# Half-size products in the gated projections of a decoder layer

## Chip, cores and metric

The kernel runs on one core of one Trainium2 chip. The metric is the device time of one execution in microseconds (us). The engines of the core work side by side, each through its own queue in order: PE (TensorE, matrix products), PEld (PE's loading of the stationary operand), DVE (VectorE), ACT (ScalarE), POOL (GpSimd) and SP (SyncE, which issues the loads and stores here). Times of single instructions come from one execution that the hardware profiler recorded.

## What is computed

One layer of a decoder on 512 tokens of width 1024, in float32:

```python
h = x + 0.5 * swiglu(rmsnorm(x, ffn1_norm), ffn1_w_in, ffn1_w_out)
h = h + hybrid_mixer(rmsnorm(h, mix_norm), ...)
h = h + 0.5 * swiglu(rmsnorm(h, ffn2_norm), ffn2_w_in, ffn2_w_out)
y = rmsnorm(h, final_norm)

def swiglu(x, w_in, w_out):            # w_in: 1024 x 5632, w_out: 2816 x 1024
    a, b = jnp.split(x @ w_in, 2, axis=-1)
    return (jax.nn.silu(a) * b) @ w_out
```

The mixer (two gated recurrences between a wide input projection and output projections) lies between the two feed-forward parts and isn't touched but for one argument.

## The kernel before

Activations lie transposed: 128 channels on the partitions, 512 tokens along a row. `h` is the residual stream in 8 such tiles. Each float32 product is made of three passes in a reduced float32 type: an operand is split into `hi` (a cast on ACT) and `lo` (operand minus `hi`, on DVE), and `mm3` (L165 to L168) multiplies hi by hi, hi by lo and lo by hi into one PSUM bank. For weights `slab` (L154) does it: SP loads 128 x 512 numbers into `raw` (3 buffers), ACT casts to `whi` (L161), DVE subtracts into `wlo` (L162), 6 buffers each. `dense` (L170) makes one block of 128 output channels from as many slabs as its depth needs: 2 slabs for 1024 channels, 24 matmuls of 512 columns.

`ffn` (L227) is called for both feed-forward parts. For each j of 22 it makes two blocks, pa and pb (the gate and the value columns of the split above), and then, on the way out of PSUM, multiplies both by `rbc` (the reciprocal root mean square of each token, L250 and L253), takes Silu of the first on ACT, multiplies them on DVE (L255) and splits the result at once into `gh` and `gl` (L256, L257). So the input of these products, `uh` and `ul`, is `h` times the norm's gain, not yet divided by the root mean square, and the statistics of a token may come late: the blocks of the first `late` pairs are made before `rbc` exists. Then 8 blocks of output follow, each from 22 tiles of gh and gl (66 matmuls), added to `h`, and `after` prepares the next norm (squares into `acc` on POOL, `uh`/`ul` of the mixer).

`opening` (L279) starts the first part with an order written out by hand (`tc.manual_schedule`): the 4 blocks of the first two pairs share their loads. `stats` (L207) sums the squares over the channels on PE, `root` (L221) takes the power -0.5 on POOL, and four small matmuls spread the result into `rbc`. Outside `manual_schedule` the build tool's own planner orders each engine's queue; the mixer, too, is written out by hand. `last` (L347) makes the last output block of the second part in two halves of 256 tokens and the final norm.

Of the kernel before, what the change touches and what calls it, by code (L numbers as in the profile page):

```python
# [16 lines left out]
P = 128  # L17
# [22 lines left out]
LATE = 1  # L40
WB = 6
EXTRA = ((1, 3, 5, 7), (1, 3, 5, 7), (1, 3, 5, 7), (5, 7))
# [82 lines left out]
def body(tc, xT, cst, sqc, hmask, dta, w1o, w1a, w2a, wt, wn, wab, wbh, wbg, wo, w1b, w2b, yT, dbg=None):  # L125
# [70 lines left out]
    def sqacc(kt, pl, tag="sqt", bufs=2, add=pool):  # L196
# [5 lines left out]
        act.activation(s, h[:, kt], AF.Square)  # L202
        if kt < KD - 1:
            add.tensor_tensor(acc, acc, s, op=ALU.add)  # L204
        return s

    def stats(pl, last, between=lambda: None):  # L207
        pt = psc.tile([P, T], F32, tag="pd", name="pst")
        for i in range(NT):
            c = slice(i * P, (i + 1) * P)  # L210
            pe.matmul(pt[:, i:i + 1], acc[:, c], ones[:, :1], start=True, stop=False)
            pe.matmul(pt[:, i:i + 1], last[:, c], ones[:, :1], start=False, stop=True)
        root(pl, pt[:, :4], rcol)
        between()
        pb = psc.tile([P, T], F32, tag="pd", name="pbc")
        for i in range(NT):
            pe.matmul(pb[:, i * P:(i + 1) * P], rcol[:, i:i + 1].to_broadcast([P, P]), ident,
                      start=True, stop=True)
        act.copy(rbc, pb)
# [7 lines left out]
    def ffn(w1, w2, c0, after, late=0, lead=None, last=None):  # L227
        with tc.tile_pool(name="ff", bufs=1) as fp:
            gh = fp.tile([P, KF, T], F32R, name="gh")
            gl = fp.tile([P, KF, T], F32R, name="gl")  # L230
            early, ahead = [], []
            if lead is not None:
                early, ahead = opening(w1, fp)
            for j in range(len(early) // 2, late):
                for n in ("fa", "fb"):
                    early.append(fp.tile([P, T], F32, name=n, bufs=3))
                    act.copy(early[-1], dense(w1[j, len(early) % 2 ^ 1], KD, ux))
            if lead is not None:
                lead()
            for j in range(KF):  # L240
                if j < late:
                    pa, pb = a, b = early[2 * j:2 * j + 2]
                    if lead is not None and j:
                        a, b = (fp.tile([P, T], F32, name=n, bufs=3) for n in ("fa", "fb"))
                    dve.tensor_tensor(a, pa, rbc, op=ALU.mult)
                    dve.tensor_tensor(b, pb, rbc, op=ALU.mult)
                else:
                    pa = ahead.pop(0) if ahead else dense(w1[j, 0], KD, ux)
                    a = fp.tile([P, T], F32, name="fa", bufs=3)
                    dve.tensor_tensor(a, pa, rbc, op=ALU.mult)  # L250
                    pb = ahead.pop(0) if ahead else dense(w1[j, 1], KD, ux)
                    b = fp.tile([P, T], F32, name="fb", bufs=3)
                    dve.tensor_tensor(b, pb, rbc, op=ALU.mult)  # L253
                act.activation(a, a, AF.Silu)
                dve.tensor_tensor(a, a, b, op=ALU.mult)  # L255
                act.copy(gh[:, j], a)  # L256
                dve.tensor_tensor(gl[:, j], a, gh[:, j].bitcast(F32), op=ALU.subtract)  # L257
            for d in range(KD if last is None else KD - 1):
                pt = dense(w2[d], KF, lambda k: (gh[:, k], gl[:, k]))
                dve.scalar_tensor_tensor(h[:, d], pt, 0.5, h[:, d], op0=ALU.mult, op1=ALU.add)  # L260
                after(d, fp)
            if last is not None:
                last(gh, gl, fp)

    def nextnorm(c0, spill=None, defer=False, **sqt):
        def after(d, pl):
            if spill is not None:
                sp.dma_start(spill[d], h[:, d])
            if c0 is not None:
                prep(d, c0)  # L270
            if defer and d == KD - 1:
                act.activation(rbc, h[:, d], AF.Square)
                return
            s = sqacc(d, pl, **sqt)
            if d == KD - 1:
                stats(pl, s)
        return after

    def opening(w, pl):  # L279

        with tc.manual_schedule(engines={x.engine for x in (pe, act, dve, pool, sp)}):
            raws = {}

            def fetch(eng, kt, c=slice(0, 512)):
                if kt not in raws:
                    raws[kt] = wp.tile([P, 512], F32, tag="raw", name="raw", bufs=RB)
                eng.dma_start(raws[kt][:, c], w1o[kt, :, c])
            act.dma_start(cs[:, :C_N], cst)
            fetch(act, 0, slice(0, 256))
            act.activation(rbc[:, :1], ones[:, :1], AF.Silu)  # L290
            sp.dma_start(h[:, 0], xT[:, 0])
            fetch(sp, 0, slice(256, 512))
            for kt in range(1, KD):
                sp.dma_start(h[:, kt], xT[:, kt])
                fetch(sp, kt)
                if kt == 4:
                    sp.dma_start(sq, sqc)

            pw = psc.tile([P, T], F32, tag="pe", name="pwarm", bufs=LANES["e"])
            for i in range(11):  # L300
                pe.matmul(pw[:, :P], ones, ones, start=True, stop=True)
            pts = [psd.tile([P, T], F32, tag="mm", name="pmm") for _ in range(2)]
            pts += [psc.tile([P, T], F32, tag="pa", name="pmm", bufs=LANES["a"]) for _ in range(2)]
            for kt in range(KD):
                prep(kt, C_F1)
                lo = wp.tile([P, 512], F32R, tag="wlo", name="wlo", bufs=WB)
                hi = wp.tile([P, 512], F32R, tag="whi", name="whi", bufs=WB)
                for c in (slice(0, 256), slice(256, 512)) if kt == 0 else (slice(0, 512),):
                    act.copy(hi[:, c], raws[kt][:, c])
                    dve.tensor_tensor(lo[:, c], raws[kt][:, c], hi[:, c].bitcast(F32), op=ALU.subtract)  # L310
                for o, pt in enumerate(pts):
                    c = slice(o * P, (o + 1) * P)
                    mm3(pt, hi[:, c], lo[:, c], uh[:, kt], ul[:, kt], kt == 0, kt == KD - 1)
                if kt:
                    sqacc(kt - 1, pl, add=dve)
            s = sqacc(KD - 1, pl)
            slabs = [slab(w[2, 0][:, :512])]
            out = []
            for pt, n in zip(pts, ("fa", "fb")):
                out.append(pl.tile([P, T], F32, name=n, bufs=3))  # L320
                act.copy(out[-1], pt)
            slabs.append(slab(w[2, 0][:, 512:]))

            more = []

            def half(n):
                if n % 2 == 0:
                    more.append(psd.tile([P, T], F32, tag="mm", name="pmm"))
                for i in range(4):
                    k, c = n % 2 * 4 + i, slice(i * P, (i + 1) * P)  # L330
                    mm3(more[-1], *(x[:, c] for x in slabs[n]), *ux(k), k == 0, k == KD - 1)

            def between():
                half(0)
                slabs.append(slab(w[2, 1][:, :512]))
            stats(pl, s, between)
            half(1)
            slabs.append(slab(w[2, 1][:, 512:]))
            half(2)
            half(3)  # L340
        return out + pts[2:], more
# [5 lines left out]
    def last(gh, gl, pl):  # L347

        scaled = (1, 3, 5)
        with tc.tile_pool(name="fo", bufs=1) as fo:  # L350
            for kt in scaled:
                act.activation(h[:, kt], h[:, kt], AF.Copy, scale=cs[:, C_FN + kt:C_FN + kt + 1])
            for q in range(2):
                c = slice(q * 256, q * 256 + 256)
                pt = dense(w2b[KD - 1], KF, lambda k: (gh[:, k, c], gl[:, k, c]), n=256)
                dve.scalar_tensor_tensor(h[:, KD - 1, c], pt[:, :256], 0.5, h[:, KD - 1, c], op0=ALU.mult, op1=ALU.add)
                s = fo.tile([P, 256], F32, name="s7", bufs=2)
                act.activation(s, h[:, KD - 1, c], AF.Square)
                ps_ = psc.tile([P, T], F32, tag="pd", name="pst")
# [4 lines left out]
                r = fo.tile([P, 2], F32, name="rl", bufs=2)  # L364
                root(fo, ps_[:, :2], r)
                pb = psc.tile([P, T], F32, tag="pe", name="pbc")
# [1321 lines left out]
```

## Time and profile before

| what | us |
|---|---|
| median of 3 runs | 1637.57 |
| lowest and highest | 1637.13, 1640.69 |
| the profiled execution | 1637.01 |
| its span, first to last instruction | 1635.2 |
| PE busy in the span | 1622.3 |
| DVE, ACT, POOL busy | 973.1, 702.1, 313.5 |
| granted TensorE clock, mean | 0.997 |

The span is what the profile's rows divide up; the execution's own time is 1.8 us longer. A row of the timeline is start, duration (us), engine, line of the kernel, operation, output<-inputs, shapes, count, and in brackets the idle time before it with what ended that. A row of a group is line, engine, operation, tiles and shapes with the count, then the busy time of the group in us and the mean of one in ns, then the idle time before them. Where a line is asked for by itself, its row gives the least, median and greatest duration in ns. A matmul's duration is longer than the distance to the next, since they overlap; the distance is its price. The first feed-forward part runs to about 370 us of the span, the mixer to about 1260, the second part from there to the end.

### The profile page before, as it was taken

The numbers are of one execution on the slowest core, as the hardware profiler recorded it, in microseconds if no ns is written. First come the engines' busy times: TensorE is split into PE (matmuls) and PEld (weight loads), VectorE is DVE, ScalarE is ACT, GpSimd is POOL, SyncE is SP. The second block draws the span as 40 slices with busy tenths as digits, with TensorE's granted clock in tenths as the row PEclk, the third lists the DMA queues.
The fourth block names the chain that finished last, engine by engine and source line by source line (L and its number), as shares of the span: only waits on it lengthen the run. The fifth ranks groups of instructions, "written<-read, shape, count | busy, mean of one in ns | idle before, by whom it ended". The sixth has DMA issues, their size and how long they took to land. (4 is left out here: it accounts for less than half of the span.)

```text
span 1635.2 us, 25919 instructions
## 1 busy us (share of the span) xinstructions
PE 1622.3 (99%) x9376; PEld 1346.7 (82%) x9376; DVE 973.1 (60%) x1961; ACT 702.1 (43%) x1582; POOL 313.5 (19%) x615
## 2 busy tenths in 40 slices
PE   9999999999999999999999999999999999999997
PEld 8888888888888888878888888888888888888886
DVE  5544443336787779758888887755544444444333
ACT  5333333323434345446666565554234433333232
POOL 0000000001221222256526656600002000000001
PEclk9999999999999999999999999999999999999998
DMA  5333333433312222443333234445634333333333
GB/s 171 111 97 97 97 94 110 118 110 97 92 53 72 85 85 91 125 146 97 97 104 123 85 110 127 138 145 181 187 107 136 95 98 97 98 97 91 97 100 103
DMA packets 107408, 178.48 MB, mean 109 GB/s; under 512 B 19584, under 2 KB 25472, under 8 KB 107280
## 3 DMA queue, kind: packets, MB, share of 16 engines
q1 hardware_dynamic: 106992, 176.60, 35.3%
q8 instruction: 74, 1.21, 0.3%
q14 instruction: 54, 0.44, 0.1%
q10 hardware_dynamic: 288, 0.22, 0.0%
HBM read 161.80 MB, written 14.97 MB: 108 GB/s over the span
## 5 line engine op out<-in xcount | busy, mean ns | idle before, releaser
L166 PE MATMUL pmm<-uh,whi 128*128 128x512 f32 x1400 | 567.6, 406 | 0.0
L168 PE MATMUL pmm<-uh,wlo 128*128 128x512 f32 x1400 | 547.0, 391 | 0.0
L167 PE MATMUL pmm<-ul,whi 128*128 128x512 f32 x1400 | 545.8, 390 | 0.0
L161 ACT CAST whi<-raw 128x512 fp32r<-128x512 f32 (+1 forms) x286 | 174.1, 610 | 392.7 <-PE pmm L167 373.8
L162 DVE TENSOR_TENSOR wlo<-raw,whi 128x512 fp32r<-128x512 f32 (+1 forms) x286 | 193.7, 678 | 239.9 <-ACT whi L161 239.6
L168 PEld LDWEIGHTS pmm<-uh,wlo 128*128 128x128 f32 x1400 | 262.8, 188 | 56.9
L166 PEld LDWEIGHTS pmm<-uh,whi 128*128 128x128 f32 x1400 | 263.2, 188 | 50.9
L167 PEld LDWEIGHTS pmm<-ul,whi 128*128 128x128 f32 x1400 | 263.5, 188 | 49.5 <-DVE ul L193 0.3
L1463 ACT CAST whi<-raw 128x512 fp32r<-128x512 f32 x226 | 140.5, 621 | 224.3 <-PE pmm L167 180.7
L1465 DVE TENSOR_TENSOR wlo<-raw,whi 128x512 fp32r<-128x512 f32 x226 | 158.6, 702 | 120.9 <-ACT whi L1463 119.3
L204 POOL TENSOR_TENSOR acc<-acc,sqt 128x512 f32<-128x512 f32 x18 | 23.3, 1297 | 774.0 <-ACT sqt L202 774.0
L166 PE MATMUL pmm<-gh,whi 128*128 128x512 f32 (+1 forms) x374 | 141.0, 377 | 0.0
L168 PE MATMUL pmm<-gh,wlo 128*128 128x512 f32 (+1 forms) x374 | 140.9, 377 | 0.0
L167 PE MATMUL pmm<-gl,whi 128*128 128x512 f32 (+1 forms) x374 | 140.8, 377 | 0.0
L168 PEld LDWEIGHTS pmm<-gh,wlo 128*128 128x128 f32 x374 | 70.4, 188 | 13.0
L166 PEld LDWEIGHTS pmm<-gh,whi 128*128 128x128 f32 x374 | 70.4, 188 | 12.9
L167 PEld LDWEIGHTS pmm<-gl,whi 128*128 128x128 f32 x374 | 70.4, 188 | 12.8
L813 DVE SCALAR_TENSOR_TENSOR cy<-ci,cs,cy 128x512 f32<-128x512 f32 x96 | 72.7, 761 | 3.2 <-ACT cy L810 2.0
L948 POOL TENSOR_TENSOR fm<-gfs,gln 128x60 f32<-128x60 f32 (+24 forms) x155 | 63.7, 411 | 55.4 <-DMA gln<-hmask 43.9
L949 POOL TENSOR_TENSOR gln<-gln,fm 128x60 f32<-128x60 f32 (+24 forms) x155 | 64.3, 415 | 12.1
L253 DVE TENSOR_TENSOR fb<-pmm,rbc 128x512 f32<-128x512 f32 x41 | 28.4, 692 | 62.3 <-PE pmm L168 62.3
L250 DVE TENSOR_TENSOR fa<-pmm,rbc 128x512 f32<-128x512 f32 x41 | 28.3, 691 | 59.7 <-PE pmm L168 59.7
(420 smaller groups left out, 2191.4 us busy)
## 6 DMA issues: line engine op xcount, KB each, us to landing
raw<-wt SPq DMA_DIRECT2D x160, 256.0 KB
raw<-w1b SPq DMA_DIRECT2D x88, 256.0 KB
raw<-w1a SPq DMA_DIRECT2D x80, 256.0 KB
raw<-w2b SPq DMA_DIRECT2D x45, 256.0 KB
raw<-w2a SPq DMA_DIRECT2D x40, 256.0 KB
raw<-wn SPq DMA_DIRECT2D x32, 256.0 KB
raw<-wbg SPq DMA_DIRECT2D x32, 256.0 KB
gb<-gtd SPq DMA_DIRECT2D x16, 256.0 KB
```

What stands on the lines that cost most here:

```text
L161: act.copy(hi[:, :f], raw[:, :f])
L162: dve.tensor_tensor(lo[:, :f], raw[:, :f], hi[:, :f].bitcast(F32), op=ALU.subtract)
L166: pe.matmul(pt, ah, bh, start=first, stop=False)
L167: pe.matmul(pt, ah, bl, start=False, stop=False)
L168: pe.matmul(pt, al, bh, start=False, stop=last)
L250: dve.tensor_tensor(a, pa, rbc, op=ALU.mult)
L253: dve.tensor_tensor(b, pb, rbc, op=ALU.mult)
L813: dve.scalar_tensor_tensor(y, ci[:, j:j + T], wc[j], y, op0=ALU.mult, op1=ALU.add)
L948: pool.tensor_tensor(tv, bc(m[:, j + 1:, j], w), t[:, j:j + 1, :w].to_broadcast([P, n, w]), op=ALU.mult)
L949: pool.tensor_tensor(t[:, j + 1:, :w], t[:, j + 1:, :w], tv, op=ALU.add)
L1463: act.copy(hi, raw)
L1465: dve.tensor_tensor(lo, raw, hi.bitcast(F32), op=ALU.subtract)
```

## The change

In both feed-forward parts most pairs (all but 4 in the first part, all but 3 in the second) are made in another way. The 256 output channels of a pair (128 of gate, 128 of value), the 1024 input channels and the 512 tokens are each cut in two, and the product of the two 2 x 2 block matrices is made by seven products of half size for eight (Winograd's form of Strassen's scheme). Each such product is 4 x 3 matmuls of 256 columns. For that

- POOL makes four sums of weight blocks a pair (`s1` to `s4`), and each of the seven weight operands is cast on ACT and subtracted on DVE;
- the seven operands on the token side are made once for each part (`operands`): the normalised input `xn` (gain and `rbc` applied), sums of its quarters, and their hi and lo;
- the products are put together on the way out of PSUM (`f0` to `f8`).

The gate's result stays in one float32 tile until the stage ends; then 17 of the 22 are cast and subtracted (`part`), into the room of the token-side operands. The other 5 are split at once into parts of `uh` and `ul`; in the first part POOL copies them away again (`move`) before the mixer's input is written there. Everything in `ffn` is now inside `manual_schedule`: `stream` runs over units (a product, or four depth tiles of an ordinary block) and issues each engine's work so many units ahead. The order of the pairs is `ORDER`; `w1o` is rearranged on the host to match. `stats` is split into `sums` and `spread`, which the stream calls between units. In the second part the statistics are taken inside the stream (`defer=True` in the mixer's last call).

```diff
-LATE = 1
 WB = 6
+RW, SW = 6, 4
+ORDER = [*range(4, 15), *range(16, 22), 0, 1, 2, 3, 15]
...
+    def stream(units, fp, early, hooks, posts):
...
+        def loads():
+            while waiting:
+                r = waiting[0]
+                n = sent[r.fast]
+                m = RW if r.fast else RB
+                if len(n) >= m and n[-m].left:
+                    break
+                r.tile = fp.tile([P, T], F32, name="rw", bufs=RW) if r.fast else \
+                    wp.tile([P, T], F32, tag="raw", name="raw", bufs=RB)
+                sp.dma_start(r.tile[:, :r.src.shape[-1]], r.src)
+                n.append(waiting.pop(0))
+
+        def ahead(comb, cast, low):
+            while todo["low"] < min(low, len(units)):
+                i = todo["low"]
+                x, hi, lo = parts[i]
+                dve.tensor_tensor(lo, x, hi.bitcast(F32), op=ALU.subtract)
+                for r in units[i].drop:
+                    r.left -= 1
+                todo["low"] += 1
+            loads()
+            while todo["comb"] < min(comb, len(units)):
+                if units[todo["comb"]].comb:
+                    units[todo["comb"]].comb()
+                    loads()
+                todo["comb"] += 1
+            while todo["cast"] < min(cast, len(units)):
...
+                act.copy(hi, x)
...
+        for t, u in enumerate(units):
+            for f in hooks.get(t, ()):
+                f()
+            u.run(*parts[t][1:])
+            for f in posts.get(t, ()):
+                f()
+            ahead(min(t, todo["cast"]) + WB + 3, min(t + WB + 1, todo["cast"] + 2), min(t + WB, todo["cast"]))
...
+    def fast(w, p, xo, fp, at, posts, gate):
...
+        def comb(n, x, y, op):
+            def f():
+                a, b = (z.tile if isinstance(z, Raw) else v[z] for z in (x, y))
+                v[n] = fp.tile([P, T], F32, name="sw", bufs=SW)
+                pool.tensor_tensor(v[n], a, b, op=op)
...
+        def sums(n, add, twice=False):
+            t, pt = fp.tile([P, T], F32, name=n, bufs=2 if n == "fa" else 1), v["pt"]
+            t2, p2, add = (x.rearrange("p (a t) -> p a t", t=256) for x in (t, pt, add))
+            dve.tensor_tensor(t2, p2, add.to_broadcast([P, 2, 256]) if twice else add, op=ALU.add)
+            return t
+        def f0():
+            act.copy(v["p1"], v["pt"][:, one[0]])
+        def f2():
+            v["ua"] = sums("fa", v["p1"], True)
+        def f3():
+            act.activation(v["ua"][:, one[1]], v["ua"][:, one[1]], AF.Silu)
+        def f4():
+            v["uu"] = sums("uu", v["ua"][:, one[0]], True)
+            dve.tensor_tensor(v["vb"], v["pt"][:, one[1]], v["uu"][:, one[0]], op=ALU.add)
+        def f6():
+            v["uc"] = sums("uc", v["uu"])
+        def f7():
+            act.activation(v["uc"][:, one[1]], v["uc"][:, one[1]], AF.Silu)
+        def f8():
+            gate(p, (ua[:, one[1]], uc[:, one[1]]), (uc[:, one[0]], v["vb"]))
...
+        return [
+            Unit([a11, a21], raw(a11), prod(0, 0, "m"), drop=(a11,)),
+            Unit([a22, a12], of("s2"), prod(2, 0, "a"), lambda: (s1(), s2())),
+            Unit([], raw(a12), prod(3, 1), drop=(a12,)),
+            Unit([], of("s1"), prod(1, 1, "b")),
+            Unit([], of("s3"), prod(4, 0), comb("s3", a11, a21, ALU.subtract)),
+            Unit([], of("s4"), prod(5, 1, "m"), comb("s4", a12, "s2", ALU.subtract)),
+            Unit([], raw(a22), prod(6, 0), drop=(a22,))]
...
+    def operands(c0, xs, rooms, start, hooks):
...
+        scaled = lambda k: lambda: dve.scalar_tensor_tensor(xn[:, k], h[:, k], cs[:, c0 + k:c0 + k + 1], rbc,
+                                                            op0=ALU.mult, op1=ALU.mult)
+        work = ((scaled(0), scaled(1)), (scaled(2), scaled(3), less(pool, t1, b12, b11)),
+                (high(0), scaled(4), scaled(5)), (scaled(6), scaled(7), low(0)),
+                (less(pool, b12, b22, b12), less(dve, t2, b22, t1), high(3), high(2)), (low(2), low(3), high(1)),
+                (low(1), less(pool, t2, b21, t2), high(4)), (low(4), high(5)), (low(5), high(6)), (low(6),))
...
+            for p in range(17):
+                on(end - 6 + p if p < 6 else end + (p - 6) // 3, part(p))
...
-    ffn(w1a, w2a, C_F1, nextnorm(C_MX, hd, defer=True), late=2, lead=lead)
+    ffn(w1a, w2a, C_F1, nextnorm(C_MX, hd, defer=True), 4, lead=lead)
...
-    ffn(w1b, w2b, C_F2, nextnorm(None), late=LATE, last=last)
+    ffn(w1b, w2b, C_F2, nextnorm(None), 3, last=last)
...
-        e["nextnorm"](C_F2, tag="ta", bufs=TA)(d, mp)
+        e["nextnorm"](C_F2, defer=True, tag="ta", bufs=TA)(d, mp)
```

`hooks` are called before a unit's matmuls are issued, `posts` behind them. In `fast`, `at` is the pair's first unit, and `f0` to `f8` are posts of the units `at` to `at + 8`, so the last two fall into the next pair. `work` in `operands` is spread over ten units from unit 2 (first part) or 3 (second part) on.

More of the change, by code (lines that the diff above doesn't have):

```diff
@@ L205, in sqacc, with stats, sums, spread @@
         return s
[L207 to L219, printed above, removed]
+    def stats(pl, last):
+        def sums():
+            pt = psc.tile([P, T], F32, tag="pd", name="pst")
+            for i in range(NT):
+                c = slice(i * P, (i + 1) * P)
+                pe.matmul(pt[:, i:i + 1], acc[:, c], ones[:, :1], start=True, stop=False)
+                pe.matmul(pt[:, i:i + 1], last[:, c], ones[:, :1], start=False, stop=True)
+            root(pl, pt[:, :4], rcol)
+        def spread():
+            pb = psc.tile([P, T], F32, tag="pd", name="pbc")
+            for i in range(NT):
+                pe.matmul(pb[:, i * P:(i + 1) * P], rcol[:, i:i + 1].to_broadcast([P, P]), ident,
+                          start=True, stop=True)
+            act.copy(rbc, pb)
+        return sums, spread
     def root(pl, ss, out):
@@ L273, in after @@
                 return
-            s = sqacc(d, pl, **sqt)
-            if d == KD - 1:
-                stats(pl, s)
-        return after
[L279 to L341, printed above, removed]
```

274 lines of the change are left out of this document (228 added, 46 removed).

## The prediction

> **What bounds the kernel now.** I read the engine totals first, then two steady stretches of the first and the second feed-forward part.
>
> ```profile
> PE 1622.3 (99%) x9376; PEld 1346.7 (82%) x9376; DVE 973.1 (60%) x1961; ACT 702.1 (43%) x1582; POOL 313.5 (19%) x615
> ```
> ```profile
> 100.00:200.00 100.00, 100.00 (x443) 82.84 (x442) 47.38 (x74) 34.25 (x55) 0.00 (x0) 1.00 0.31 98
> 1400.00:1500.00 100.00, 100.00 (x443) 82.84 (x442) 47.42 (x73) 34.22 (x55) 0.00 (x0) 1.00 0.31 96
> ```
>
> The columns of the window rows are length, then PE, PEld, DVE, ACT and POOL busy, clock, DMA share, GB/s. PE never pauses at full clock, DVE has half its time free, ACT two thirds, POOL is unused. So in these stages the time is the number of matmuls times their pitch, which the timeline gives. The first pair of rows is 52 pitches apart, the second 63.
>
> ```profile
> 100.09 0.39 PE L167 MATMUL pmm<-ul,whi 128*128 128x512 f32 x1
> ...
> 111.88 0.39 PE L168 MATMUL pmm<-uh,wlo 128*128 128x512 f32 x1
> ```
> ```profile
> 1605.50 0.28 PE L166 MATMUL pmm<-gh,whi 128*128 128x256 f32 x1
> ...
> 1613.06 0.28 PE L166 MATMUL pmm<-gh,whi 128*128 128x256 f32 x1
> ```
>
> 512 columns: 11.79/52 = 0.2267 us. 256 columns: 7.56/63 = 0.120 us, 6% more than half.
>
> **The products on PE.** A pair of column blocks now takes 2 x 8 x 3 = 48 wide matmuls, 10.88 us. By seven half products it takes 7 x 4 x 3 = 84 narrow ones, 10.08 us. An eighth less work is worth 0.80 us a pair, not 1.36. There are 18 fast pairs in the first part, 19 in the second: 37 x 0.80 = 29.6 us, if nothing else ends later. The Trainium skill (TensorE: Matmul & The Clock Gate, section "Wait — 56ns, not 53.3ns?") gives the warm pitch as columns over 2.4 GHz plus some 2.5 ns, for bf16; by an estimate from it the gain would be 48 x 0.2158 - 84 x 0.1092 = 1.19 us a pair, 44 us. The rows here are slower at both widths, and they decide.
>
> **What the pair adds elsewhere.** Before: 4 casts on ACT and 4 subtractions on DVE for the weights, 4 operations on DVE and 2 on ACT for the gate, nothing on POOL. After: POOL makes 4 sums of weight blocks (512 wide); ACT 7 casts, a copy and two half-width Silus; DVE 7 subtractions for the low parts, three 512-wide and one 256-wide sum out of PSUM, and two 256-wide gate products. DVE's pitch in a queue that is never empty:
>
> ```profile
> 18.39 0.74 DVE L193 SCALAR_TENSOR_TENSOR ul<-h,cs,uh 128x512 fp32r<-128x512 f32 x1
> 19.05 0.68 DVE L310 TENSOR_TENSOR wlo<-raw,whi 128x512 fp32r<-128x512 f32 x1
> 19.65 0.69 DVE L204 TENSOR_TENSOR acc<-acc,sqt 128x512 f32<-128x512 f32 x1
> ...
> 1614.08 0.42 DVE L356 SCALAR_TENSOR_TENSOR h<-pmm,h 128x256 f32<-128x256 f32 x1
> 1614.42 0.42 DVE L162 TENSOR_TENSOR wlo<-raw,whi 128x256 fp32r<-128x256 f32 x1
> ```
> ```profile
> L161 ACT CAST whi<-raw 128x512 fp32r<-128x512 f32 x37 | 23.1, 623 | 50.5 <-PE pmm L167 50.2 <-PE pmm L168 0.3
> ```
>
> So 0.60 us for 512, 0.34 for 256, 0.66 for the form with three operands. DVE: 10 x 0.60 + 3 x 0.34 = 7.05 us a pair; ACT at most 7 x 0.62 + 3 x 0.42 = 5.6. Both fit into 10.08. But POOL and DVE are not independent:
>
> ```profile
> 295.30 1.29 POOL L204 TENSOR_TENSOR acc<-acc,sqt 128x512 f32<-128x512 f32 x1 [13.69 <-ACT sqt L202]
> ```
> ```profile
> 296.38 0.76 DVE L162 TENSOR_TENSOR wlo<-raw,whi 128x512 fp32r<-128x512 f32 x1 [0.96 <-ACT whi L161]
> 299.10 0.69 DVE L162 TENSOR_TENSOR wlo<-raw,whi 128x512 fp32r<-128x512 f32 x1 [1.96 <-ACT whi L161]
> ```
> ```profile
> 1607.26 1.29 POOL L204 TENSOR_TENSOR acc<-acc,sqt 128x512 f32<-128x512 f32 x1 [13.66 <-ACT sqt L202]
> ```
> ```profile
> L162 DVE TENSOR_TENSOR wlo<-raw,whi x286: 415/692/1386, 20.3 to 1614.4; 128x512 fp32r<-128x512 f32 x143
> ```
>
> The subtraction of 296.38 ends at 297.14, 0.55 after POOL's end at 296.59. The longest one (1386 ns) is that of 1607.71: it ends at 1609.10, again 0.55 after POOL's end at 1608.55. So DVE's subtraction of two SBUF tiles spends 0.14 us on its start, then stands still until POOL has finished its sum, then streams 0.55. POOL likewise waits for DVE, and they take turns:
>
> ```profile
> 536.61 1.75 POOL L637 TENSOR_TENSOR ke<-ke,fl 128x256 f32<-128x256 f32 x2 [2.62 <-DVE ah L646]
> ```
> ```profile
> 536.93 0.90 DVE L1465 TENSOR_TENSOR wlo<-raw,whi 128x512 fp32r<-128x512 f32 x1
> 537.75 0.90 DVE L696 TENSOR_TENSOR qp<-qp,fl 128x256 f32<-128x256 f32 x1
> ```
>
> The first subtraction ends 537.83, the second POOL operation 0.53 later (538.36), DVE's next 0.29 after that. An operation with one input in PSUM isn't held:
>
> ```profile
> 428.00 0.69 DVE L587 TENSOR_TENSOR fs<-pmm,rbc 128x512 f32<-128x512 f32 x1
> ```
> ```profile
> 428.24 1.64 POOL L637 TENSOR_TENSOR ke<-ke,fl 128x256 f32<-128x256 f32 x2 [2.37 <-PE pl L688]
> ```
>
> **One pair with these rows.** POOL's four sums hold the port 1.29 - 0.14 = 1.15 us each. The first of them reuses the buffer of the first sum one pair earlier, whose last reader is the low part of product 4. So the four start after that subtraction, one after another, taking turns with DVE. DVE's order from there: a PSUM sum (not held), low, low, gate half, gate half, low, PSUM sum, low, low, two PSUM sums, low, low. The first POOL sum runs from 0.22 to 1.37; the PSUM sum hides 0.44 of it, and DVE waits 0.71. The other three each come in between two held operations, 1.09 us of waiting each. DVE: 7.05 + 0.71 + 3 x 1.09 = 11.03, say 11.05 us a pair. Nothing hidden gives 7.05 + 4 x 1.2 = 11.9; all 2.15 us of PSUM sums hidden gives 9.7, below PE. I take 11.05: the written order puts one PSUM sum beside POOL, and the rows show turns without exception. That is above PE's 10.08 and above the old 10.88. Up to six products of lead (six buffers) put it off for two or three pairs, not for eighteen.
>
> The waits that this adds: DVE's sums wait for a product on PE, and the low parts queued behind them are what PE waits for five products later; ACT's Silus wait for those sums with casts behind them; SP's loads wait for POOL's sums and DVE's subtractions with the next loads behind. With DVE late, the products they wait for are long done, so only DVE's own length counts.
>
> Loads: the same four blocks of 256 KB a pair, on SP.
>
> ```profile
> 1607.71 2.13 DVE L162 TENSOR_TENSOR wlo<-raw,whi 128x512 fp32r<-128x512 f32 x2 [0.99 <-ACT whi L161]
> ```
> ```profile
> 1611.89 0.62 ACT L161 CAST whi<-raw 128x512 fp32r<-128x512 f32 x1 [1.33 <-DMA raw<-w2b]
> ```
>
> From a freed buffer (1609.10) to the cast that waits for the load is 2.8 us. A fast buffer is freed about 2.8 us before POOL needs its successor, so I cost loads at nothing; 0.5 us late would add 0.3 a pair.
>
> **Normalising first.** It begins when rbc is there; in the first part as now:
>
> ```profile
> 33.39 0.59 ACT L219 COPY rbc<-pbc 128x512 f32<-128x512 f32 x1 [5.19 <-PE pbc L217]
> ```
> ```profile
> 33.11 0.48 PE L166 MATMUL pmm<-uh,whi 128*128 128x512 f32 x1
> ```
>
> From 34.0 DVE has, up to the last operand: 8 scalings (5.3 us), 8 operations of 1024 columns (not in the trace; twice 0.55 plus 0.06, an estimate: 9.2), 9 low parts (5.4), 9 column operations and a sum (6.0): 25.9 us. POOL's holds in that stretch: three for pair 0 and six weight sums (9 x 1.15), three operand differences (3 x 2.3, twice the row): 17.2 us, of which I take three quarters, 13, as DVE's loss, since seven of its operations read PSUM. The last operand is ready at 73; PE, with seven wide half columns of 2.72 us from 33.11 and six products after them, would want it at 60.8: 12 us lost (2 if POOL cost nothing here, 15 if all). In the second part four half columns more lie in between: 25.9 + 9.5 + 2 of waiting from 7 us on, against 41.8: 3 us (0 to 6).
>
> **The end of the stage.** The 17 gate casts and subtractions now come at once. The last pair has no POOL sums, so DVE gains there and PE sets 10.08; the kept g of pairs 17 to 19 costs 0.6 each. DVE then needs some 4.5 us around unit 2 of the output product, against 2.72: PE waits 1.4 us.
>
> **At nothing**: the ten POOL copies that move the kept pairs (at most 1.29 each) lie under the second output column (66 x 0.2267 = 15 us); the reordered w1o and other tags change no count; the tail runs the same chain. At the seam to the mixer, its casts now come ahead of the last output column's work:
>
> ```profile
> 367.76 0.63 ACT L1463 CAST whi<-raw 128x512 fp32r<-128x512 f32 x1 [0.69 <-PE pmm L167]
> 368.71 0.73 ACT L192 ACTIVATE uh<-h,cs 128x512 fp32r<-128x512 f32 x1 [0.33 <-DVE h L260]
> ```
>
> If a written order on both sides forbids that, ACT, load (2.8) and low part follow PE's end: up to 5 us. I take 0 by the row and keep 5.
>
> **The sum.** First part: 16 x 11.05 + 2 x 10.08 + 1.8 + 12 + 1.4 = 212.2 against 18 x 10.88 = 195.8: +16.4. Second: 17 x 11.05 + 20.2 + 1.8 + 3 + 1.4 = 214.2 against 206.7: +7.5. Together +23.9 on the profiled execution's 1637.0 us (span 1635.2; the median of the runs is 1637.6): 1661.
>
> **Rivals.** *PE keeps the lead* (faster): of POOL's 4.6 us a pair at least 1.6 fall beside PSUM sums or idle DVE. Then a pair is 10.08, the operands come just in time, and 29.6 less 0 to 5 at the seams gives about 1609. For it: DVE's 30% free time, six buffers of lead. Against: the order above, which hides 0.6; it decides at 1.6. *Half hidden*: a late load pushes POOL's block under the later PSUM sums, 10.5 a pair: 33 x 0.55 = 18 less, 1643, or 1637 with half the operand loss. *Nothing hidden*, or the seam's 5 us: 33 x 0.85 = 28 more, 1689.
>
> **How the numbers follow.** Forecast 0.60 (own range 1648 to 1680), PE's lead 0.22, half hidden 0.10, nothing hidden 0.08. 1610 to 1684 leaves out nearly half of the second case and most of the last, under 0.2. Measurement tells 0.2%, 3.3 us, apart. Faster 0.24 (the second case and a little of the third), same 0.07, slower 0.69.
>
> **What would show it.** In the fast stage: DVE near 90% busy with subtractions well over 1 us on average ("busy" includes the standing still), PE gaps ended by DVE's wlo, pairs 11 us apart. Wrong, if PE is busy throughout at 0.120 a matmul: then the turns cost less than I say. A POOL sum far from 1.29, or one that starts elsewhere in DVE's order, breaks the walk; gaps at the first products mean operands, at units 2 and 3 of the output product the casts.

## The result, and the profile after

The changed kernel takes 1681.45 us (median of 4 runs, 1680.95 to 1684.88) against 1637.35 us before (4 runs, 1636.94 to 1640.69): ratio 1.0269, 95% interval 1.025 to 1.0288, 44 us slower. The forecast was 1661, range 1610 to 1684: the right side, but only just inside the stated range and 1.5 us outside the narrower 1648 to 1680 that went with the forecast itself; nearly half of the loss is missing.

First the totals of the page after, then the same two stretches as before (length, then PE, PEld, DVE, ACT, POOL busy, clock, DMA share, GB/s):

```profile
PE 1617.8 (96%) x10708; PEld 1395.8 (83%) x10708; DVE 1266.9 (75%) x2212; ACT 768.9 (46%) x1779; POOL 572.0 (34%) x782
```
```profile
100.00:200.00 100.00, 92.46 (x748) 90.07 (x747) 99.69 (x116) 41.77 (x89) 54.91 (x36) 1.00 0.32 95
1400.00:1500.00 100.00, 93.74 (x748) 90.43 (x748) 99.69 (x118) 41.66 (x88) 51.02 (x36) 1.00 0.31 93
```

Totals say little: PE still has 96%. The stretches say it: PE has gaps now, and DVE has none. What DVE does there is seen in the timeline of one pair, from one sum `uc` to the next (start, duration, both us; "x2" is two operations back to back), and in POOL's rows of the same time:

```profile
148.82 0.68 DVE L346 TENSOR_TENSOR uc<-px,uu 128x512 f32<-128x512 f32 x1
149.42 2.06 DVE L282 TENSOR_TENSOR wlo<-sw,whi 128x512 fp32r<-128x512 f32 x2
151.40 1.52 DVE L426 TENSOR_TENSOR rooma<-fa,uc 128x256 f32<-128x256 f32 x1
152.84 1.51 DVE L426 TENSOR_TENSOR rooma<-uc,vb 128x256 f32<-128x256 f32 x1
154.27 0.68 DVE L282 TENSOR_TENSOR wlo<-rw,whi 128x512 fp32r<-128x512 f32 x1
154.87 0.68 DVE L346 TENSOR_TENSOR fa<-px,p 128x512 f32<-128x512 f32 x1
...
156.67 0.68 DVE L346 TENSOR_TENSOR uu<-px,fa 128x512 f32<-128x512 f32 x1
157.38 0.42 DVE L362 TENSOR_TENSOR vb<-px,uu 128x256 f32<-128x256 f32 x1
157.72 1.82 DVE L282 TENSOR_TENSOR wlo<-rw,whi 128x512 fp32r<-128x512 f32 x1
159.47 0.68 DVE L282 TENSOR_TENSOR wlo<-sw,whi 128x512 fp32r<-128x512 f32 x1
160.07 0.68 DVE L346 TENSOR_TENSOR uc<-px,uu 128x512 f32<-128x512 f32 x1
```
```profile
149.03 1.30 POOL L327 TENSOR_TENSOR sw<-sw,rw 128x512 f32<-128x512 f32 x1 [0.68 <-POOL sw L327]
150.95 1.68 POOL L327 TENSOR_TENSOR sw<-rw 128x512 f32<-128x512 f32 x1 [0.63 <-DVE wlo L282]
152.60 1.47 POOL L327 TENSOR_TENSOR sw<-rw,sw 128x512 f32<-128x512 f32 x1
157.70 1.29 POOL L327 TENSOR_TENSOR sw<-rw 128x512 f32<-128x512 f32 x1 [3.64 <-DMA rw<-w1a]
```

Four places are long, one for each POOL sum. The two subtractions of 149.42 take 2.06 instead of 1.28, the gate products 1.52 and 1.51 instead of 0.42, the subtraction of 157.72 takes 1.82 instead of 0.68: 0.78 + 1.10 + 1.09 + 1.14 = 4.11 us of standing still. The sums out of PSUM (`fa`, `uu`, `uc`) take 0.68 whatever POOL does. A gate product has half the columns and stands just as long: the price is that of the POOL operation, not of its own. The page's groups show the same over the whole run, and who pays (busy, mean ns of one, idle before and what ended it):

```profile
L169 PE MATMUL px<-xs,wlo 128*128 128x256 f32 x1036 | 301.3, 291 | 30.1 <-DVE wlo L282 29.9
```
```profile
L282 DVE TENSOR_TENSOR wlo<-sw,whi 128x512 fp32r<-128x512 f32 x148 | 146.8, 1010 | 0.0
```

Where the 44 us arise is read from PE's rows at the seams: the first output product of the first part, the statistics behind it, the first output product of the second part, and the statistics behind that. Before:

```profile
248.10 0.39 PE L166 MATMUL pmm<-gh,whi 128*128 128x512 f32 x1
...
370.51 0.28 PE L1546 MATMUL pst<-ones,acc 128*128 128x1 f32 x2
...
1500.78 0.39 PE L166 MATMUL pmm<-gh,whi 128*128 128x512 f32 x1
...
1622.66 0.28 PE L361 MATMUL pst<-ones,acc 128*128 128x1 f32 x2
```

After:

```profile
271.45 0.40 PE L167 MATMUL pmm<-uh,whi 128*128 128x512 f32 x1
...
396.98 0.28 PE L1792 MATMUL pst<-ones,acc 128*128 128x1 f32 x2
...
1543.43 0.40 PE L167 MATMUL pmm<-uh,whi 128*128 128x512 f32 x1
...
1669.33 0.28 PE L600 MATMUL pst<-ones,acc 128*128 128x1 f32 x2
```

The differences are 23.4, 26.5, 42.7 and 46.7 us; the span ends 44.5 later. So the projections of the first part lose 23.4, those of the second 42.7 - 26.5 = 16.2 (with the mixer between them), the output products 3.1 and 4.0; the tail gives 2.2 back.

### The profile page after: what moved, and what is told of

It is laid out like the page before. It is cut to its first block, busy times and chain, and to the rows that moved or that the text cites. A ratio compares the mean times of both kernels' runs of the same rounds, so it can differ in the third digit from the quotient of the medians.

```text
span 1679.7 us, 29400 instructions
## 1 busy us (share of the span) xinstructions
PE 1617.8 (96%) x10708; PEld 1395.8 (83%) x10708; DVE 1266.9 (75%) x2212; ACT 768.9 (46%) x1779; POOL 572.0 (34%) x782
## 4 chain that ended last, share of the span: by engine, by line
PE 69%; DVE 24%; issue 4%; ACT 2%; DMA 1%; SPq 0%; POOL 0%; DVEq 0%; POOLq 0%; ACTq 0%
PE pmm L167 18%; PE pmm L169 17%; PE pmm L168 17%; DVE wlo L282 11%; DVE rooma L426 3%; DVE roomb L426 2%; PE pnat L167 2%; PE pnat L169 2%; PE pnat L168 2%; DVE uc L346 1%; DVE uu L346 1%; DVE fa L346 1%; DVE g L426 1%; DVE xs L397 1%; PE pog L1357 1%
## 5 line engine op out<-in xcount | busy, mean ns | idle before, releaser
L167 PE MATMUL pmm<-uh,whi 128*128 128x512 f32 (+1 forms) x863 | 358.6, 416 | 3.1 <-DVE uc L440 3.1
L169 PE MATMUL pmm<-uh,wlo 128*128 128x512 f32 (+1 forms) x863 | 337.8, 391 | 0.0
L168 PE MATMUL pmm<-ul,whi 128*128 128x512 f32 (+1 forms) x863 | 336.5, 390 | 0.0
L169 PE MATMUL px<-xs,wlo 128*128 128x256 f32 x1036 | 301.3, 291 | 30.1 <-DVE wlo L282 29.9
L167 PE MATMUL px<-xs,whi 128*128 128x256 f32 x1036 | 296.6, 286 | 7.9 <-DVE fa L440 4.2
L168 PE MATMUL px<-xs,whi 128*128 128x256 f32 x1036 | 296.6, 286 | 5.3 <-DVE xs L397 5.3
L169 PEld LDWEIGHTS px<-xs,wlo 128*128 128x128 f32 x1036 | 201.7, 195 | 39.5 <-DVE wlo L282 39.3
L167 PEld LDWEIGHTS px<-xs,whi 128*128 128x128 f32 x1036 | 201.9, 195 | 8.9 <-ACT xs L396 6.3
L168 PEld LDWEIGHTS px<-xs,whi 128*128 128x128 f32 x1036 | 201.9, 195 | 6.4 <-DVE xs L397 6.4
L327 POOL TENSOR_TENSOR sw<-rw 128x512 f32<-128x512 f32 x74 | 120.4, 1627 | 151.0 <-DMA rw<-w1b 60.5
L282 DVE TENSOR_TENSOR wlo<-sw,whi 128x512 fp32r<-128x512 f32 x148 | 146.8, 1010 | 0.0
L167 PE MATMUL pmm<-xs,whi 128*128 128x512 f32 (+1 forms) x238 | 90.1, 379 | 3.0 <-ACT xs L485 3.0
L168 PE MATMUL pmm<-xs,whi 128*128 128x512 f32 (+1 forms) x238 | 90.2, 379 | 1.7 <-DVE xs L486 1.7
```

What stands on the lines that cost most here:

```text
L167: pe.matmul(pt, ah, bh, start=first, stop=False)
L168: pe.matmul(pt, ah, bl, start=False, stop=False)
L169: pe.matmul(pt, al, bh, start=False, stop=last)
L282: dve.tensor_tensor(lo, x, hi.bitcast(F32), op=ALU.subtract)
L327: pool.tensor_tensor(v[n], a, b, op=op)
```

## The experiments

**The theory** that the first four runs test is that of the prediction: DVE bounds the fast stage because it stands still in turns with POOL. Rival A: it is DVE's own work and its place in the order; POOL only lies beside it. Rival B: the weight blocks are loaded too late (POOL waited 60.5 us for `w1b` alone).

**The sums on DVE.**

```diff
-                pool.tensor_tensor(v[n], a, b, op=op)
+                dve.tensor_tensor(v[n], a, b, op=op)
```

> The four sums of weight blocks of every fast pair move from POOL to DVE; nothing else changes. Theory (DVE is the bound of the fast stage because it stands still in turns with POOL's sums): DVE's work a pair becomes 7.05 + 4 x 0.60 = 9.45 us with nothing to stand still for, below PE's 10.08, so pairs come 10.08 apart instead of 11.22 and PE is busy 97% or more in the stretch from 100 to 200 us. 37 x 1.14 = 42 us less, and some of the loss at the operands back: 1622 to 1642 us. Rival A (DVE's own work and its place in the order is the bound, POOL only lies beside it): DVE gets 2.4 us more a pair, 13.6 apart, 37 x 2.4 = 89 us more: about 1770. Rival B (the loads of weight blocks come late, POOL waits 60 us for them): pairs stay 11.2 apart, 1675 to 1690.

1637.68 us (8 runs, before 1638.1), ratio 0.9999, interval 0.9988 to 1.0011: 2.4 us a pair of *more* work on the engine that is the bound, and 44 us less.

```profile
100.00:200.00 100.00, 100.00 (x835) 100.00 (x835) 97.46 (x172) 53.85 (x101) 0.00 (x0) 1.00 0.34 108
```
```profile
139.25 0.69 DVE L346 TENSOR_TENSOR uc<-px,uu 128x512 f32<-128x512 f32 x1
...
209.81 0.69 DVE L346 TENSOR_TENSOR uc<-px,uu 128x512 f32<-128x512 f32 x1
```

Seven pairs in 70.56 us: 10.08 apart, as 84 x 0.120 asks, and PE doesn't pause. The same low parts that took 1010 ns on average now take

```profile
L282 DVE TENSOR_TENSOR wlo<-sw,whi 128x512 fp32r<-128x512 f32 x148 | 102.1, 710 | 0.0
```

Both rivals fall: A wanted 1770, B 1675 or more.

**No sums at all.**

```diff
-            Unit([a22, a12], of("s2"), prod(2, 0, "a"), lambda: (s1(), s2())),
+            Unit([a22, a12], raw(a11), prod(2, 0, "a"), drop=(a11,)),
...
-            Unit([], of("s4"), prod(5, 1, "m"), comb("s4", a12, "s2", ALU.subtract)),
+            Unit([], raw(a22), prod(5, 1, "m"), drop=(a22,)),
```

> The four sums of weight blocks are left out; the products that read a sum read one of the four raw blocks instead, so the projections are not those of the reference. Casts, subtractions, products, loads and everything behind are as many as before. Theory (turns with POOL): DVE has 7.05 us a pair, PE sets 10.08; 42 us less in the fast stages and the six sums gone from the time of the operands: 1610 to 1635. Rival A (DVE's own work): pairs stay about 11.2 apart, 1675 to 1685. Rival B (late loads): the same four loads a pair in the same buffers, pairs stay at 11.2, 1675 to 1690.

This kernel leaves out all four sums: the products read raw weight blocks in their place, so what it computes isn't the layer, and only its time is of use. 1620.41 us (one run), pairs 10.08 apart, DVE 73% busy and PE 100% between 100 and 200 us. DVE's own work is far from a bound, and the same loads keep up.

**Two and two.**

```diff
-                pool.tensor_tensor(v[n], a, b, op=op)
+                (dve if n in ("s1", "s2") else pool).tensor_tensor(v[n], a, b, op=op)
```

> The first two sums of a pair on DVE, the last two on POOL. Theory (turns): DVE has 7.05 + 1.20 = 8.25 us of its own and stands still at most 2 x 1.09 us: 10.43 a pair, 0.79 less than now, 37 x 0.79 = 29 less: 1645 to 1657; where one of the two falls beside a sum out of PSUM, down to 10.08 and 1635. Rival A: 1.2 us more a pair, 1725. Rival B: 1675 to 1690.

1666.08 us (one run), 9 over the range. Eight pairs lie between these rows, 10.67 apart:

```profile
93.51 0.69 DVE L346 TENSOR_TENSOR uc<-px,uu 128x512 f32<-128x512 f32 x1
...
178.86 0.69 DVE L346 TENSOR_TENSOR uc<-px,uu 128x512 f32<-128x512 f32 x1
```

That is 0.24 over the 10.43: the two operations that need the result of the one just ahead of them start 0.72 behind it instead of 0.60. With all sums on DVE it is the same: there `vb` at 88.61 starts 0.72 after `uu` at 87.89, and the second weight sum at 83.60 starts 0.72 after the first at 82.88. That is 2 x 0.12, missing in my 9.45, which came to 9.67 where DVE set the pace; of my 7.05 one 0.12, that of `vb`, is missing.

**One sum twice.**

```diff
-                pool.tensor_tensor(v[n], a, b, op=op)
+                for _ in range(2 if n == "s2" else 1):
+                    pool.tensor_tensor(v[n], a, b, op=op)
```

> POOL makes the second of its four sums twice, the same one into the same buffer; all else as it is. Theory (turns): one more hold of 1.15 us a pair between two held operations, up to 1.09 us a pair: 37 x 1.09 = 40 more, 1722, less where it falls beside a sum out of PSUM: 1705 to 1725. Rival A (DVE's own work): POOL is idle 45 of 100 us in the fast stage and takes it for nothing: 1681 to 1686. Rival B (late loads): the block that the sum reads isn't freed later than its own low part, 1681 to 1690.

1715.42 us (one run): 34 more, for an operation on an engine that was idle for 45 of 100 us. Eleven pairs of the first part lie between these rows, 12.01 apart, 0.79 more:

```profile
106.36 0.68 DVE L347 TENSOR_TENSOR uc<-px,uu 128x512 f32<-128x512 f32 x1
...
238.45 0.68 DVE L347 TENSOR_TENSOR uc<-px,uu 128x512 f32<-128x512 f32 x1
```

With none, two, four and five sums on POOL and the order otherwise kept, pairs come 10.08 (9.67 where DVE leads), 10.67, 11.22 and 12.01 apart. The turns are the mechanism of the fast stage.

**What was left open** after these: with the sums on DVE the products should have given 29.6 us, and gave none. PE stands 10 us between 40 and 80 us there, where the operands are made, and the granted clock of that stretch is 0.87. The other six runs take that apart.

**More wide pairs, sums on POOL.** Each part begins with more pairs by the old products, while the operands are made.

```diff
-    ffn(w1a, w2a, C_F1, nextnorm(C_MX, hd, defer=True), 4, lead=lead)
+    ffn(w1a, w2a, C_F1, nextnorm(C_MX, hd, defer=True), 6, lead=lead)
...
-    ffn(w1b, w2b, C_F2, nextnorm(None), 3, last=last)
+    ffn(w1b, w2b, C_F2, nextnorm(None), 4, last=last)
```

> Sums on POOL as in the changed kernel; two more pairs of the first part and one more of the second go by the old wide products (6 and 4 instead of 4 and 3) ahead of the fast ones. Theory (DVE is the bound from the normalising to the end of the stage, so its own sum of work sets both parts): a wide pair costs DVE 8 x 0.60 = 4.8 us instead of 11.22, 6.4 less each, three times: 1681.5 - 19 = 1662 (1658 to 1668). Rival (the operands cost no time of their own, only the distance of the fast pairs counts): 3 x (11.22 - 10.88) = 1 less, 1680.

1663.19 us (one run), 18 less, where the theory had 19 and its rival 1: *fewer* fast products and a faster kernel.

**The same with the sums on DVE** (both edits above):

> Sums on DVE, and 6 and 4 pairs by wide products. With the sums on DVE, PE still stands 10 us between 40 and 80 us and 3.4 us between 1300 and 1320. Theory: these are the operands, which DVE makes behind the column operations; three wide pairs give it 3 x (9.67 - 4.8) = 14.6 us, PE pays 3 x 0.80 = 2.4: 1637.7 - 13.4 + 2.4 = 1627 (1624 to 1631). Rival (the loss is made of what the order puts there whatever stands before it): 1637 to 1640.

1625.75 us (3 runs, before 1637.26), ratio 0.9934, interval 0.9911 to 0.9956. As the theory has it; this is the first version below both kernels, 0.7% below the one before the change.

**The low part of a kept gate product one unit later.**

```diff
                     act.copy(hi, g)
-                    dve.tensor_tensor(lo, g, hi.bitcast(F32), op=ALU.subtract)
+                    return lambda: dve.tensor_tensor(lo, g, hi.bitcast(F32), op=ALU.subtract)
...
-            gate(p, (ua[:, one[1]], uc[:, one[1]]), (uc[:, one[0]], v["vb"]))
+            v["keep"] = gate(p, (ua[:, one[1]], uc[:, one[1]]), (uc[:, one[0]], v["vb"]))
+
+        def f9():
+            if v["keep"]:
+                v["keep"]()
-        for t, f in ((0, f0), (2, f2), (3, f3), (4, f4), (6, f6), (7, f7), (8, f8)):
+        for t, f in ((0, f0), (2, f2), (3, f3), (4, f4), (6, f6), (7, f7), (8, f8), (9, f9)):
```

> As the one before, and the low part of a kept gate product (pairs 17 to 21) is made one unit later, so that DVE doesn't stand behind ACT's cast. With the sums on DVE these pairs come 11.05 apart, 1.38 more than DVE's 9.67 without them. Theory: 0.78 of that is DVE's waiting for the cast, 0.60 the operation; pairs 10.27 apart, ten of them, 7.8 us less of DVE where it is the bound, and PE's waits at the output product go: 4 to 9 us less than the one before, 1618 to 1623. Rival (the lead of six products covers it anyway): within 1 us of the one before.

1625.57 us (3 runs), 0.2 less: the rival held. Three of the kept pairs do come closer (10.45 instead of 11.05), but the last takes 12.7 instead of 12.1, so DVE gains 1.2 and 1.3 us in the two parts instead of 3.9 each. That PE's lead of six products covers most of the rest is my reading of it: ahead of these pairs DVE keeps up, at 10.08 a pair. A miss, and a useful one: a stall on an engine that has got ahead again costs little.

**Nearly the order alone.** 16 of 22 pairs wide, in both parts.

> As the one before, but 16 pairs of each part by wide products, and only the last 6 by the seven half products: nearly the written order, the normalising and the moves by themselves. Theory (these cost nothing where DVE isn't the bound): 1637.6 - 12 x 0.80 = 1628 (1626 to 1632). Rival (order, moves or seams cost time of their own): above 1633, with PE standing at the seams.

1640.19 us (8 runs), ratio 1.0022, interval 1.0011 to 1.0034: 12 us above the theory. The windows say where:

```profile
40.00:80.00 40.00, 36.07 (x150) 28.79 (x149) 33.37 (x37) 17.75 (x26) 10.65 (x4) 0.96 0.29 98
...
240.00:280.00 40.00, 38.06 (x205) 32.31 (x204) 31.48 (x51) 22.73 (x43) 8.55 (x10) 1.00 0.32 96
```

PE stands 3.9 us at the operands and 1.9 at the output product; in the second part, from 1280 to 1320 and from 1480 to 1520, 2.0 and 2.3: 10.1 in all. The theory fails: even where few products are fast, PE waits at these seams. Its longest wait, 3.28 us, is for a column operation of DVE, and the waits at the output product are for gate casts on ACT and low parts on DVE. The clock in the first row is 0.96, an estimated 1.6 us more (0.04 x 40): see the last section.

**The same operand steps, spread out.** Started from the kernel with late low parts.

```diff
-            hooks.setdefault(start + t, []).extend(fs)
+            hooks.setdefault(start + t * 4 // 3, []).extend(fs)
```

> As the kernel with sums on DVE, more wide pairs and late low parts (1625.6), but the ten steps that make the operands come over 13 units instead of ten. There PE stands 5.4 us between 40 and 80 us and 2.0 us between 1280 and 1320, mostly for column operations that free a PSUM tile and that DVE has queued behind scalings and low parts of operands. Theory (a queue too dense, not too long): spread out, PE's waits shrink to 0 to 3 us in all: 1619 to 1623. Rival (POOL's three operand differences make it, each holding DVE over 2 us, wherever they stand): within 1.5 us of 1625.6.

1618.76 us (4 runs, before 1638.32), ratio 0.9883, interval 0.9867 to 0.99: 6.8 less.

```profile
40.00:80.00 40.00, 36.40 (x167) 29.81 (x166) 36.71 (x42) 18.49 (x28) 12.33 (x4) 1.00 0.34 110
```

PE stands 3.6 us here instead of 5.4, a little over the 0 to 3 of the theory, and not at all between 1280 and 1320 us instead of 2.0: 3.7 less. The clock accounts for the rest: it is 1.00 in both stretches and was 0.96 in both before, an estimated 3.2 us (0.04 x 80). So the rival falls, but the theory explains only about half of the gain.

**And the three operand differences on DVE.**

```diff
-        work = ((scaled(0), scaled(1)), (scaled(2), scaled(3), less(pool, t1, b12, b11)),
+        work = ((scaled(0), scaled(1)), (scaled(2), scaled(3), less(dve, t1, b12, b11)),
...
-                (less(pool, b12, b22, b12), less(dve, t2, b22, t1), high(3), high(2)), (low(2), low(3), high(1)),
-                (low(1), less(pool, t2, b21, t2), high(4)), (low(4), high(5)), (low(5), high(6)), (low(6),))
+                (less(dve, b12, b22, b12), less(dve, t2, b22, t1), high(3), high(2)), (low(2), low(3), high(1)),
+                (low(1), less(dve, t2, b21, t2), high(4)), (low(4), high(5)), (low(5), high(6)), (low(6),))
```

> As the one before, and the three operand differences of 1024 columns on DVE instead of POOL. In the kernel that both start from, DVE stands still some 6 us beside these three (4.21 instead of 1.28 for two low parts, 2.25 and 2.30 instead of 0.68 for one), and would have 3 x 1.14 = 3.4 us of its own work instead. Theory: 0 to 3 us less than the one before. If POOL's differences are the cause (rival of the one before): 3 to 6 us less than the one before.

1615.95 us (4 runs), ratio 0.9865, interval 0.9851 to 0.988: 22 us faster than before, 65 faster than the change, and the fastest of all. The stretch of the operands, in the kernel before these two edits and with both:

```profile
40.00:80.00 40.00, 34.65 (x144) 27.36 (x142) 34.85 (x40) 17.39 (x26) 10.64 (x4) 0.96 0.29 94
```
```profile
40.00:80.00 40.00, 37.50 (x174) 30.70 (x173) 34.90 (x47) 18.98 (x29) 1.30 (x1) 1.00 0.35 112
```

PE is busy 2.9 us longer in the same 40 us and the clock is full, with DVE busy just as long: the queue was too dense. What POOL's differences add to that is small and not well measured. The medians are 2.8 us apart, inside the 0 to 3 of the expectation and just short of its rival's 3 to 6; but the two profiled executions are 0.6 apart, and PE stands 2.5 us in this stretch against 3.6 without the second edit. To 1637.6 - 34 x 0.80 = 1610.4 there remain 5.5 us, which PE's standing covers: 2.5 us here, 2.0 and 1.7 at the two output products. Nothing was tried against the waits at the output products.

## Why the prediction was right in direction and short by half

**What bounds the kernel, and the products on PE: right.** 10.08 a pair where nothing else is late, in six kernels, against 10.88 for a wide pair: the 0.80 of the rows. The 1.19 us a pair estimated from the Trainium skill (TensorE: Matmul & The Clock Gate, section "Wait — 56ns, not 53.3ns?") isn't borne out.

**The walk through a pair: right to 2%, and in one place by luck.** The forecast was 11.05 a pair.

```profile
81.20 0.68 DVE L346 TENSOR_TENSOR uc<-px,uu 128x512 f32<-128x512 f32 x1
...
227.35 0.68 DVE L346 TENSOR_TENSOR uc<-px,uu 128x512 f32<-128x512 f32 x1
...
276.11 0.68 DVE L346 TENSOR_TENSOR uc<-px,uu 128x512 f32<-128x512 f32 x1
```

Thirteen distances of 11.24 on average (median 11.22). The standing still was 4.11 against 3.98 forecast; the rest is the 0.12 of `vb`. But POOL's sums don't stand where the walk put them. It started all four behind the low part of product 4 (159.47 in the timeline above). The first sum starts ahead of that, at 157.70, after 3.64 us of waiting for its load, and holds the low part of product 3 for 1.14; it is the second one that runs beside a sum out of PSUM (149.03 beside 148.82) and costs 0.78. One of the four is partly hidden either way, so the total came out. DVE was 99.7% busy, not "near 90%": by my own reckoning, with the standing still counted as busy, nothing should have been left. And the subtractions took 0.88 us (`rw`) and 1.01 us (`sw`) on average, not well over 1.

**The end of the fast stage: too small.** I wrote 0.6 for each of three kept products and 10.08 for the last two pairs, 3.7 us over the last four distances. They are five, four of them between 227.35 and 276.11, and these 48.8 us are 8.4 over four times 10.08. A kept product costs more than its own 0.6:

```profile
243.95 1.51 DVE L426 TENSOR_TENSOR g<-uc,vb 128x256 f32<-128x256 f32 x1
246.15 0.69 DVE L430 TENSOR_TENSOR ul<-g,uh 128x512 fp32r<-128x512 f32 x1 [0.68 <-ACT uh L429]
```

DVE waits 0.68 for ACT's cast between the two. I had priced the operation and not the trip to ACT and back.

**Normalising first: the term that failed.** It was forecast at 12 us in the first part and 3 in the second. Measured from the row 81.20: the wide products end at 52.4, the first pair needs 10.08, so its `uc` could begin at 62.5 and begins 18.7 later. In the second part the same sum, from the start that the first part's loss leaves (1500.78 - 22 x 10.88 + 26.5 = 1287.9, with 32.6 of wide products and 10.08 behind it), gives 1330.6; `uc` begins at 1342.35, 11.7 later. Together 15.4 us more than forecast, the largest part of the missing 20. (The end of the stage, 4.7 too small in each part, is given back by the 4.7 and 4.8 us by which PE is ahead of DVE there, which the forecast hadn't counted.) The first part adds up: 18.7 here, 13 x 1.16 = 15.1 in the walk and 8.4 at its end, less the 4.7 by which DVE's last `uc` (276.11) trails the last product (271.45), are 37.5, against 23.4 + 18 x 0.80 = 37.8 at the seam.

Three steps were short, as the groups of DVE from 34 to 81 us show:

```profile
L399 DVE SCALAR_TENSOR_TENSOR rooma<-h,cs,rbc 128x512 f32<-128x512 f32 x8 | 8.7, 1130 | 0.0
L282 DVE TENSOR_TENSOR wlo<-rw,whi 128x512 fp32r<-128x512 f32 x5 | 7.5, 1494 | 0.0
L282 DVE TENSOR_TENSOR wlo<-sw,whi 128x512 fp32r<-128x512 f32 x6 | 6.7, 1124 | 0.0
...
L282 DVE TENSOR_TENSOR wlo<-raw,whi 128x512 fp32r<-128x512 f32 x3 | 3.8, 1288 | 0.0
```

First, the count: 14 low parts, 11 of them ahead of the last operand; I counted nine. Second, the loss to POOL: the eight scalings took 8.7 where I had 5.3, one low part 2.51 beside a 1024-column difference; up to the last operand each operation's excess over its length without POOL adds up to some 15 us in the timeline, where I took 13. (The bounds that I gave, 2 us lost if POOL cost nothing and 15 if all, don't follow from my own sum, which gives 0 and 16.) With 1.8 us in which DVE itself stood idle, these put the last operand at 78.1 instead of 73. Third, and this the count of DVE's time could not show, a sum of work says when the last operand is ready, not what waits on the way. In the second part I had DVE 2.6 us behind PE (7 + 25.9 + 9.5 + 2 against 41.8). There the last operand was late too, and before it was needed PE had already waited for two column operations that stood in DVE's queue behind steps of the operands:

```profile
1318.04 0.47 PE L167 MATMUL pmm<-uh,whi 128*128 128x512 f32 x1 [3.10 <-DVE uc L440]
...
1327.65 0.36 PE L167 MATMUL px<-xs,whi 128*128 128x256 f32 x1 [2.25 <-issue]
```

The view names no engine for the second wait; DVE's column operation `fa` ended 0.10 us ahead of its end. With 1.39 us for a low part at 1336.69 these waits are 6.7 of the 11.7. How much is due to the density of the queue alone isn't shown for this kernel; in the later ones with the sums on DVE, spreading the same steps took 3.7 us off PE's waits.

**The output product: too small.** 1.4 forecast, 3.1 and 4.0 measured, of which PE waited 2.2 and 2.5 for gate casts on ACT and low parts on DVE. **At nothing: right.** The moves, the loads (the wait of POOL's first sum for its load changes only where DVE is held) and the seam to the mixer: both kernels make twelve matmuls of the mixer between the last output product and the statistics, without a pause, so the shift of 26.5 was there when the output product ended. The tail even gave 2.2 back.

**The rivals.** "PE keeps the lead" didn't happen as long as POOL had the sums, and the trace shows why: of POOL's 4.6 us a pair 0.5 was hidden, where it took 1.6. With POOL out of it and the operands spread, the case came true, at 1616 instead of its 1609, with 34 fast pairs instead of 37. "Half hidden" wanted 10.5 a pair and "nothing hidden" 11.9; at 11.22 neither happened. That the measured time is nearer to the 1689 of the latter than to 1661 comes from the seams, chiefly the operands, not from the pairs.

## What to carry to other kernels

Idle time on an engine is no free capacity where its operations and the bounding engine's exclude each other: price an operation on POOL at what it takes from DVE (1.1 us here, against 0.60 for doing it on DVE itself). When work is put in front of a stage, compare not its sum with the time available but each short operation that the bounding engine needs with what has been queued ahead of it, and spread the long ones. An algorithm that saves an eighth of the products can be worth more when applied to fewer of them, if the others give the preparation time to run: here 34 pairs did better than 37, with the weight sums on POOL and with them on DVE.

## What the runs showed of the hardware

**The turns.** An operation of DVE with two SBUF inputs stood for some 1.1 us beside each POOL sum, whether it has 512 columns (0.68 alone) or 256 (0.42 alone); one with an input in PSUM took 0.68 throughout. The Trainium skill (SBUF — State Buffer, section "Who interferes with whom") has it so: the two engines share a read interface, and a DVE instruction with at most one SBUF input, outside its 2-port modes, doesn't contend. The trace agrees.

**A wait of PE can cost more than its length.** After waiting 4.22 us for a column operation, the changed kernel's narrow matmuls come 0.214 apart instead of 0.120:

```profile
56.79 0.55 PE L167 MATMUL px<-xs,whi 128*128 128x256 f32 x1 [4.22 <-DVE fa L440]
57.14 0.41 PE L168 MATMUL px<-xs,whi 128*128 128x256 f32 x1
...
59.28 0.41 PE L169 MATMUL px<-xs,wlo 128*128 128x256 f32 x1
```

Ten pitches from 57.14 to 59.28. The granted clock was 0.76 between 60 and 80 us. But the length of the wait doesn't decide. In the kernel with late low parts, wide matmuls came 0.43 apart instead of 0.227 after a wait of 3.31 us (four pitches from 56.26 to 57.97), and also about a microsecond after one of 1.97 us (six pitches from 1294.35 to 1296.91):

```profile
1293.08 0.47 PE L167 MATMUL pmm<-uh,whi 128*128 128x512 f32 x1 [1.97 <-DVE fa L444]
...
1294.35 0.63 PE L169 MATMUL pmm<-uh,wlo 128*128 128x512 f32 x1
...
1296.91 0.63 PE L169 MATMUL pmm<-uh,wlo 128*128 128x512 f32 x1
```

In the kernel before it, with the sums on DVE and more wide pairs, a wait of 3.29 us at the same place cost nothing more; the nine matmuls from 56.26 to 58.38 take 2.12 us, 0.24 each:

```profile
56.26 0.47 PE L167 MATMUL pmm<-uh,whi 128*128 128x512 f32 x1 [3.29 <-DVE fa L440]
...
58.38 0.39 PE L167 MATMUL pmm<-uh,whi 128*128 128x512 f32 x1
```

The clock of the stretch from 40 to 80 us was 0.96 in the former and 1.00 in the latter; it was 1.00 with the spread steps too, where PE waited 2.70 us at once, and in the fastest version, where its longest wait there was 1.4 us. That is the other half of what spreading gave, and a price that the prediction had nowhere. The Trainium skill (TensorE: Matmul & The Clock Gate, section "What's actually happening") describes a gate that halves the clock after an idle window of about 3.4 us. The trace agrees with the halving, 0.227 to 0.43; a slow stretch after 1.97 us and none after 3.29 us don't fit a limit of that length on a single wait, and what else decides was not tested.

**Dependence has a price.** In the kernel with all sums on DVE, an operation of DVE that reads what the one just ahead of it writes (512 columns in both cases seen) starts 0.72 us after that one's start (82.88 and 83.60, 87.89 and 88.61), not 0.60.
